# Re-cutting the eight PSUM banks of an encoder layer: three large and two small tiles in place of two and four

## The chip, the cores and the metric

One core of one Trainium2 chip runs the whole program in one launch. Five engines work side by side, each through its own instruction stream in order: PE multiplies matrices and writes only to PSUM, ScalarE (ACT) and VectorE (DVE) read PSUM and do the elementwise work, GpSimd (POOL) works on SBUF alone, and SyncE (SP) issues the DMAs. PSUM here is eight banks of 128 partitions x 512 float32 values, and a program divides them into tiles that are taken and given back. The metric is the device time of one execution in microseconds (us), as a median of several runs.

## What is computed

One layer of an encoder with three gated branches, applied to two requests with the same weights: the "prompt" of 1024 tokens and the "sample" of 512, at width 1024. All of it is float32.

```python
def encoder_layer(x, mem, ...):
    h = rms_norm(x, ln_pre)
    z = h @ w_in                                   # 1024 -> 6400 columns
    (pool_in, pool_gate, q, k, v, attn_gate, xq, x_gate, merge_logits) = split(z)
    pool_out  = multiscale_pool(pool_in, w_pool, pool_scale)
    attn_out  = self_attention(rope(rms(q)), rope(rms(k)), v)      # 8 heads of 64, 2 kv heads
    cross_out = cross_attention(xq, rms_norm(mem, ln_mem), w_mem_kv)   # 4 heads of 128, 256 memories
    branches = (pool_out * silu(pool_gate), attn_out * silu(attn_gate), cross_out * silu(x_gate))
    gates = sigmoid(merge_logits + b_merge)
    merged = sum(gates[n] * (branches[n] @ w_branch[n]) for n in range(3))
    return x + rms_norm(merged @ w_out, ln_post)
```

## The kernel before

**Products in three parts.** Every float32 operand is kept as a high part in a rounded float32 form that PE takes at its fast rate, and a low part that is the rest. `mm3` (L132) makes one product of three matmuls: high by high, high by low, low by high. ACT writes the high part, DVE subtracts for the low one (`split`, L164). A matmul is 128x128 by 128x512 where nothing else is said, and its result fills one bank.

**PSUM tiles.** Two tags share the eight banks. `A` (L91) gives tiles of 1024 values, two banks each, and there are two of them. `B` (L94) gives tiles of 512, one bank each, and there are four. A planner runs over the traced program before it is compiled: it puts each engine's instructions into an order by priority (mostly the order of the source, moved ahead where the code says `tc.high_priority`), hands out tiles of a tag as they come free, and inserts the waits. On the chip the order of each engine is then fixed.

**The stages, in order of time.**

- *Start* (to about 97 us). `mem_phase` (L660) makes keys and values of the memories into A tiles. Between its steps it advances `long_h` (L232), which normalises the prompt's 1024 tokens in two halves: `mean_squares` and `spread` (L209) put each token's factor along a row of 512 in a B tile, and `scaled` (L254) multiplies it in, straight from that B tile (L257). It then builds seven combinations of blocks, `h[0]` to `h[6]`, with DVE subtractions.
- *Block products* (about 68 to 584 us). `products` (L318) takes weight tiles two by two for the prompt and makes their 2x2 blocks with seven block products in place of eight. Each is 12 matmuls. They add into three sums named in the string `"XYXZXZX"` (L363): X takes the products 0, 2, 4 and 6, Y takes 1, Z takes 3 and 5. All three are B tiles (L367). A pair takes about 20 us, X is open all that while, and ACT or DVE reads X in between (`keep`, `both`). After each product one step of a background task runs: tails that transpose k, q and v (A for the first transposes, B named `tp` for the second) and the pooling tail (B named `o`).
- *Bare products of the sample* (about 582 to 690 us). `plain` (L393) makes one product of 24 matmuls at a time into a B tile, for the first pairs of the sample; its tails run as background.
- *Attention* (about 690 to 1148 us). `stream` (L888) steps through units: 64 of the prompt's self-attention, 8 of its cross-attention, 16 pairs of units of the sample, 4 of its cross-attention. For each unit `scores` (L771) takes an A tile, fills it with 4 matmuls, DVE takes the row maximum (L782) and ACT the exponential (L784), which is the last reader. Two units later `turn` (L789) takes an A tile for 8 transposes, and ACT and DVE split it (L800). Two units later again `values` (L802) adds 8 matmuls of 256 columns into a B tile `o` that is held over two units; ACT and DVE read it out (L882, L883). `weave` (L108) puts halves of the sample's remaining `plain` products between the units, as a filling.
- *Merge and output* (about 1156 us to the end), three blocks of 512 tokens. `merge` (L981) makes 24 products of 12 matmuls into B tiles `pj` (L989), which DVE reads at L996. `out_phase` (L1003) takes A tiles for the first half of the columns and B, B and A for the second; `ending` (L1063) finishes the last quarter with a B tile for each of four token tiles (L1073).

Small SBUF tiles of 128x512 come from the tag `hu` (L85, eight buffers), large ones from `med` (fourteen).

Of the kernel before, what the change touches and what calls it, by code (L numbers as in the profile page):

```python
# [61 lines left out]
def encoder_kernel(ctx: ExitStack, tc, wt, xs, xts, mt, cols, rows, rope, edge, ys):  # L62
# [12 lines left out]
    def nm(s):  # L75
        count[0] += 1
        return f"{s}_{count[0]}"
# [11 lines left out]
        return sb.tile([P, D], F32, tag="raw", bufs=NRAW, name=nm("raw"))  # L89

    def A(dt=F32):  # L91
        return ps.tile([P, 1024], dt, tag="A", bufs=2, name=nm("A"))

    def B(dt=F32):  # L94
        return ps.tile([P, 512], dt, tag="B", bufs=4, name=nm("B"))

    def S(n):
        return st.tile([P, n], F32, tag=f"s{n}", bufs=3 if n == 16 else 8, name=nm("s"))
# [110 lines left out]
    def spread(r, out=None):  # L209

        dg = U()[:, :BLK]
        shape = [P, TT, P]
        v.tensor_tensor(dg.rearrange("p (t m) -> p t m", t=TT), ident[:].unsqueeze(1).broadcast_to(shape),
                        r.unsqueeze(2).broadcast_to(shape), op=ALU.mult)
        b = B()
        cost[0] += 3 * BLK / 2.4
        mm(b[:], ones[:], dg, start=True, stop=True)
        if out is None:
            return b[:]
        with tc.high_priority(EVAC):  # L220
            act.activation(out, b[:], AF.Copy)
# [10 lines left out]
    def long_h(xt, h):  # L232

        h += [[None] * 4 for _ in range(7)]
        xv = xt.rearrange("p (k t) -> p k t", k=KC)
        q = [[M(F32) for _ in range(2)] for _ in range(2)]
        for j in range(2):
            for i in range(2):
                load(q[i][j][:].rearrange("p (c n) -> p c n", c=4), xv[:, i * 4:i * 4 + 4, j * BLK:(j + 1) * BLK])
        yield  # L240
        r, sp, sq = S(16), [], []
        for j in range(2):
            sq.append([squares(q[i][j][:]) for i in range(2)])
            yield
        for j in range(2):
            rj = r[:, j * TT:(j + 1) * TT]
            mean_squares(sq[j], rj)
            rstd_of(rj)
            yield
            sp.append(spread(rj))  # L250
            yield
        b11, b12, b21, b22 = [[q[i][j][:, :D], q[i][j][:, D:]] for i in range(2) for j in range(2)]

        def scaled(i, j):  # L254
            for c in range(4):
                x = q[i][j][:, c * BLK:(c + 1) * BLK]
                v.scalar_tensor_tensor(x, x, colt[:, i * 4 + c:i * 4 + c + 1], sp[j], op0=ALU.mult, op1=ALU.mult)  # L257

        def put(k, x):
            for c in range(2):  # L260
                parts_of(h[k], 2 * c, x[c])

        def difference(out, a, b):
            for c in range(2):
                v.tensor_tensor(out[c], a[c], b[c], op=ALU.subtract)

        scaled(0, 0)
        put(0, b11)
        yield
        scaled(1, 0)  # L270
        put(1, b21)
        yield
        scaled(0, 1)
        scaled(1, 1)
        yield
        t3, t4 = (U(), U()), (U(), U())
        difference(t3, b22, b12)
        difference(b12, b12, b11)
        difference(b11, b22, b12)
        put(2, b11)  # L280
        put(3, b12)
        put(4, t3)
        put(5, b22)
        difference(t4, b21, b11)
        put(6, t4)
# [32 lines left out]
    def products(pairs, h, n, background):  # L318

        ops = {}  # L320

        def prepare():
            for p, (k0, k1, _) in enumerate(pairs):
                r0, r1 = RAW(), RAW()
                load(r0[:], wt[TILES[k0]])
                load(r1[:], wt[TILES[k1]])
                a11, a12, a21, a22 = r0[:, :BLK], r0[:, BLK:], r1[:, :BLK], r1[:, BLK:]
                ta, tb = SUM(), SUM()
                s2, s1, s3, s4 = ta[:, :BLK], ta[:, BLK:], tb[:, :BLK], tb[:, BLK:]
                with tc.high_priority(AHEAD):  # L330
                    v.tensor_tensor(s1, a21, a22, op=ALU.add)
                    v.tensor_tensor(s2, s1, a11, op=ALU.subtract)
                    v.tensor_tensor(s3, a11, a21, op=ALU.subtract)
                    v.tensor_tensor(s4, a12, s2, op=ALU.subtract)
                for i, x in enumerate((r0[:], ta[:], tb[:], a22)):
                    hi, lo = [w[:, :x.free_size()] for w in WT()]
                    with tc.high_priority(AHEAD):
                        split(hi, lo, x)
                    for k in range(2 if i < 3 else 1):
                        ops[p, 2 * i + k] = [w[:, k * BLK:(k + 1) * BLK] for w in (hi, lo)]  # L340
                    yield

        prep = prepare()
        done = 0

        def ready(i):
            nonlocal done
            while done < i and next(prep, prep) is not prep:
                done += 1

        for p, (_, _, take) in enumerate(pairs):
            banks = {}
            kept = {}

            def keep(k, b):
                kept[k] = HU()
                with tc.high_priority(EVAC):
                    act.activation(kept[k][:, :n], b, AF.Copy)

            def both(i, j, b, k):  # L360
                take(i, j, b, kept.pop(k)[:, :n])

            for i, bank in enumerate("XYXZXZX"):  # L363
                ready(p * 4 + i // 2 + LOOK)
                start = bank not in banks
                if start:
                    banks[bank] = B()  # L367
                b = banks[bank][:, :n]
                w = ops.pop((p, i))
                for c in range(4):  # L370
                    s = slice(c * P, (c + 1) * P)
                    mm3(b, (w[0][:, s], w[1][:, s]), h[i][c], start and c == 0, c == 3,
                        skip_group_check=True)
                    if c == 1:
                        yield
                if i == 0:
                    keep("p1", b)
                elif i == 1:
                    both(0, 0, b, "p1")
                elif i == 2:  # L380
                    keep("p16", b)
                elif i == 3:
                    keep("p5", b)
                elif i == 4:
                    both(1, 1, b, "p5")
                elif i == 5:
                    both(0, 1, b, "p16")
                else:
                    take(1, 0, b, None)
                next(background, None)  # L390
                yield

    def plain(pairs, h, background):  # L393

        for k0, k1, take in pairs:
            for i, key in enumerate((k0, k1)):
                w, b = weights(*key), B()
                for k in range(KC):
                    mm3(b[:], w(slice(k * P, (k + 1) * P)), h[k], k == 0, k == KC - 1)
                    if k == 3:  # L400
                        next(background, None)
                        yield
                take(i, 0, b[:], None)
                next(background, None)
                yield

    def summed(b, s, out=None):

# [572 lines left out]
    def merge(n, gd, bs, br, acc, merged):  # L981

        if not acc:
            acc += [M(F32), M(F32)]
        for d in range(KC):
            w = weights("branch", n, d // 2) if d % 2 == 0 else w
            sg = HU()
            load(sg[:], gd[n][d][:, bs])
            pj = B()  # L989
            for k in range(4):  # L990
                mm3(pj[:], w(slice((d % 2) * 512 + k * P, (d % 2) * 512 + (k + 1) * P)), br[k], k == 0, k == 3)
            yield
            at = acc[d // 4][:, (d % 4) * BLK:(d % 4 + 1) * BLK]
            with tc.high_priority(EVAC):
                o = at if n == 0 else sg[:]
                v.scalar_tensor_tensor(o, sg[:], 1.0, pj[:], op0=ALU.add, op1=ALU.mult)  # L996
            if n > 0:
                pool.tensor_tensor(at, at, sg[:], op=ALU.add)  # L998
            if merged is not None and d % 2:
                merged.extend(split_pair(acc[d // 4][:, (d % 4 - 1) * BLK:(d % 4 + 1) * BLK]))  # L1000
            yield
# [61 lines left out]
    def ending(merged, src, dst, yv, ssq, lnpost):  # L1063
# [6 lines left out]
        for t in range(TT):  # L1070
            x = U()
            load(x, src[t * P:(t + 1) * P, :])
            o = B()[:, :256]  # L1073
            for k in range(KC):
                ts = slice(t * P, (t + 1) * P)
                s = slice(k % 4 * 256, k % 4 * 256 + 256)
# [24 lines left out]
    run(drained(products(pairs[-4:], h, BLK, bg)))  # L1101
    run(pre)
    scs, kts, vts, pairs, bg, _, drained = group(0)
    run(plain(pairs[0], hs, bg))
    merged = []
    fill = drained(plain(pairs[1], hs, bg))
    units = [u for b in range(2) for u in attention(b, sc, kt, vt)]
    units += [u for b in range(2) for u in cross(b, sc, mkd[1], mvd[1])]
    units += pairs_of(scs, kts, vts) + cross(0, scs, mkd[0], mvd[0])
# [103 lines left out]
```

## Time and profile before

| | |
|---|---|
| median of three runs | 1495.29 us (1495.1 to 1495.49) |
| profiled execution, device time | 1496.65 us |
| its span, first to last instruction | 1494.8 us |
| work outside that span | 1.85 us |
| mean granted TensorE clock | 0.989 |
| PE busy / weight loads (PEld) | 1456.0 us / 1210.1 us |
| DVE / ACT / POOL busy | 976.5 / 709.6 / 273.3 us |

A row of a group or of the timeline gives engine, line, operation, tile written <- tiles read, shape and count. Matmuls overlap: one of 512 columns is shown with some 390 ns, while the next starts about 0.23 us after it, so starts tell more than lengths. PEld is the load of a matmul's stationary operand, which runs ahead of the matmul. Brackets at the end of a timeline row, and the last column of the waits, tell how long an engine was idle and what ended it.

### The profile page before, as it was taken

To read this page: it belongs to the slowest core of one execution; us is meant where nothing else is said; L and a number is where in the kernel's file an instruction comes from. 1 tells how busy PE (TensorE), PEld (TensorE's weight loads), DVE (VectorE), ACT (ScalarE), POOL (GpSimd) and SP (SyncE) were. 2 spreads that over 40 slices of the span, in tenths; PEclk is the share of its full clock that TensorE was granted. 3 is DMA by queue.
4 is the path that set the end of the run, shared out by engine and by line. 5 is a ranking of instruction groups with operands and counts; after the bars stand their busy time and mean duration, and the time that the engine had idled before them with its cause. 6 is when DMAs were issued, how large, how long until landed. Compare 5 with 4: busy or idle time off the path is not lost.

```text
span 1494.8 us, 19564 instructions
## 1 busy us (share of the span) xinstructions
PE 1456.0 (97%) x7264; PEld 1210.1 (81%) x7264; DVE 976.5 (65%) x1215; ACT 709.6 (47%) x1083; POOL 273.3 (18%) x286
## 2 busy tenths in 40 slices
PE   7979999999999999999999999999998999999998
PEld 5768888888888888887888888888886888888887
DVE  6996586666648564747767666676775664764764
ACT  6444444544434545434656556566675233323332
POOL 1000020110000000301222222234232150250241
PEclk9989999999999999999999999999999999999999
DMA  7513233332422434344222223165446844954952
GB/s 277 172 47 106 85 114 125 108 132 66 129 92 78 158 133 128 102 150 148 64 96 80 91 68 106 58 219 173 155 155 214 286 148 132 347 193 140 336 163 84
DMA packets 88174, 211.37 MB, mean 141 GB/s; under 512 B 9872, under 2 KB 19216, under 8 KB 87312
## 3 DMA queue, kind: packets, MB, share of 16 engines
q1 hardware_dynamic: 88080, 210.14, 42.7%
q8 instruction: 57, 0.93, 0.3%
q14 instruction: 37, 0.30, 0.1%
HBM read 155.57 MB, written 54.53 MB: 141 GB/s over the span
## 4 chain that ended last, share of the span: by engine, by line
PE 85%; DMA 4%; DVE 4%; ACT 4%; issue 2%; SPq 1%; POOL 0%; DVEq 0%; POOLq 0%; ACTq 0%
PE B L126 66%; PE A L126 14%; PE A L130 5%; ACT u L784 1%; DVE s L782 1%; ACT whi L165 1%; DMA raw<-wt 1%; DVE wlo L162 1%; PE B L130 1%; DMA hu<-xq 1%; ACT med L165 1%; SPq L139 1%; DMA u<-x_prompt 0%; DMA hu<-merge 0%; DMA hu<-x_gate 0%
## 5 line engine op out<-in xcount | busy, mean ns | idle before, releaser
L126 PE MATMUL B<-med,whi 128*128 128x512 f32 x2776 | 871.2, 394 | 15.8 <-ACT med L165 15.8
L126 PEld LDWEIGHTS B<-med,whi 128*128 128x128 f32 x2776 | 515.8, 189 | 122.2 <-ACT med L165 17.5
L126 PE MATMUL B<-med,wlo 128*128 128x512 f32 x1388 | 544.1, 392 | 0.6 <-DVE wlo L162 0.6
L126 PEld LDWEIGHTS B<-med,wlo 128*128 128x128 f32 x1388 | 261.9, 189 | 56.6 <-DVE wlo L162 1.7
L162 DVE TENSOR_TENSOR wlo<-raw,whi 128x1024 fp32r<-128x1024 f32 (+1 forms) x169 | 213.3, 1263 | 141.6 <-ACT whi L165 140.7
L165 ACT ACTIVATE whi<-raw 128x1024 fp32r<-128x1024 f32 (+1 forms) x169 | 167.5, 991 | 288.5 <-PE B L126 198.3
L165 ACT ACTIVATE med<-A 128x1024 fp32r<-128x1024 f32 x92 | 94.3, 1025 | 108.4 <-PE A L130 108.2
L162 DVE TENSOR_TENSOR med<-A,med 128x1024 fp32r<-128x1024 f32 (+1 forms) x93 | 113.0, 1215 | 42.0 <-ACT med L165 40.8
L187 POOL TENSOR_SCALAR s<-s 128x16 f32<-128x16 f32 (+3 forms) x17 | 6.9, 404 | 669.0 <-DVE s L556 333.2
L786 POOL TENSOR_SCALAR u<-u,s 128x1024 f32<-128x1024 f32 x64 | 72.1, 1127 | 251.3 <-DVE s L785 219.1
L130 PE MATMUL A<-ident,u 128*128 128x128 f32 x784 | 102.8, 273 | 0.9 <-DVE med L162 0.2
L130 PEld LDWEIGHTS A<-ident,u 128*128 128x128 f32 x784 | 90.1, 140 | 16.3 <-issue 5.2
L998 POOL TENSOR_TENSOR med<-med,hu 128x512 f32<-128x512 f32 x48 | 77.0, 1617 | 142.3 <-DVE hu L996 142.2
L782 DVE TENSOR_REDUCE s<-A 128x1 f32<-128x1024 f32 x64 | 78.1, 1220 | 32.9 <-PE A L126 11.3
L126 PE MATMUL A<-kt,med 128*128 128x512 f32 x320 | 91.9, 409 | 2.7 <-ACT u L784 1.2
L126 PE MATMUL A<-whi,med 128*128 128x512 f32 (+1 forms) x320 | 92.4, 368 | 0.2 <-ACT hu L1027 0.2
L784 ACT ACTIVATE u<-A,s 128x1024 f32<-128x1024 f32 x64 | 71.3, 1114 | 38.4 <-DVE s L782 38.0
L165 ACT ACTIVATE whi<-sum 128x1024 fp32r<-128x1024 f32 x50 | 53.1, 1062 | 65.6 <-PE B L126 63.7
L162 DVE TENSOR_TENSOR med<-med,med 128x1024 fp32r<-128x1024 f32 (+1 forms) x50 | 55.8, 1127 | 38.1 <-ACT med L165 34.2
L165 ACT ACTIVATE med<-med 128x1024 fp32r<-128x1024 f32 (+1 forms) x44 | 44.2, 1017 | 74.8 <-POOL med L998 36.2
L162 DVE TENSOR_TENSOR wlo<-sum,whi 128x1024 fp32r<-128x1024 f32 x50 | 61.1, 1221 | 23.3 <-ACT whi L165 22.4
L126 PE MATMUL B<-med,vt 128*128 128x256 f32 x512 | 75.9, 287 | 0.4 <-ACT med L165 0.4
(179 smaller groups left out, 1610.4 us busy)
## 6 DMA issues: line engine op xcount, KB each, us to landing
raw<-wt SPq DMA_DIRECT2D x168, 512.0 KB, 3.7
merge<-hu SPq DMA_DIRECT2D x72, 256.0 KB, 2.0
hu<-merge SPq DMA_DIRECT2D x72, 256.0 KB, 5.2
med<-br SPq DMA_DIRECT2D x36, 256.0 KB, 5.6
q<-hu SPq DMA_DIRECT2D x24, 256.0 KB, 2.6
br<-hu SPq DMA_DIRECT2D x24, 256.0 KB, 2.3
med<-q SPq DMA_DIRECT2D x12, 512.0 KB, 5.0
med<-xt_prompt SPq DMA_DIRECT2D x4, 1024.0 KB, 13.2
```

Source lines behind the costliest of these rows:

```text
L126: pe.matmul(out, l, r, **k)
L130: pe.transpose(out, x, i[:])
L139: return nc.sync.dma_start(out, src)
L162: v.tensor_tensor(out, x, hi.bitcast(F32), op=ALU.subtract)
L165: act.activation(hi, x, AF.Copy)
L187: pool.tensor_scalar(ss, ss, EPS, 1.0, op0=ALU.add, op1=ALU.mult)
L782: v.reduce_max(mx[:], a[:], axis=AX.X, negate=True)
L784: act.activation(p, a[:], AF.Exp, bias=mx[:], accum_out=sm[:])
L786: pool.tensor_scalar(p, p, rc[:], 1.0, op0=ALU.mult, op1=ALU.mult)
L998: pool.tensor_tensor(at, at, sg[:], op=ALU.add)
```

## The change

Five edits, all on who takes which PSUM tile. The tag A gets three tiles and B two: again eight banks. In `long_h` the spread factors are copied by ACT into an `hu` tile each and `scaled` reads them there. In `products` X takes the first half of an A tile, Y and Z stay with B. `plain` gets its tile from a function that the caller passes: before the attention B and A in turn, within it always B. `merge` and `ending` take B and A in turn.

```diff
     def A(dt=F32):
-        return ps.tile([P, 1024], dt, tag="A", bufs=2, name=nm("A"))
+        return ps.tile([P, 1024], dt, tag="A", bufs=3, name=nm("A"))
 
     def B(dt=F32):
-        return ps.tile([P, 512], dt, tag="B", bufs=4, name=nm("B"))
+        return ps.tile([P, 512], dt, tag="B", bufs=2, name=nm("B"))
...
             yield
-            sp.append(spread(rj))
+            sp.append(HU())
+            spread(rj, sp[j][:])
             yield
...
-                v.scalar_tensor_tensor(x, x, colt[:, i * 4 + c:i * 4 + c + 1], sp[j], op0=ALU.mult, op1=ALU.mult)
+                v.scalar_tensor_tensor(x, x, colt[:, i * 4 + c:i * 4 + c + 1], sp[j][:], op0=ALU.mult, op1=ALU.mult)
...
                 if start:
-                    banks[bank] = B()
-                b = banks[bank][:, :n]
+                    banks[bank] = (A() if bank == "X" else B())[:, :n]
+                b = banks[bank]
...
-    def plain(pairs, h, background):
+    def plain(pairs, h, background, bank):
...
-                w, b = weights(*key), B()
+                w, b = weights(*key), bank(i)
...
+    def single(i):
+        return B()
+
+    def either(i):
+        return (A() if i % 2 else B())[:, :BLK]
...
-            pj = B()
+            pj = either(d)
...
-            o = B()[:, :256]
+            o = either(t)[:, :256]
...
-    run(plain(pairs[0], hs, bg))
+    run(plain(pairs[0], hs, bg, either))
     merged = []
-    fill = drained(plain(pairs[1], hs, bg))
+    fill = drained(plain(pairs[1], hs, bg, single))
```

## The prediction

> **What bounds the kernel now.** I read the page first, then the busy time by stage.
>
> ```profile
> span 1494.8 us, 19564 instructions
> PE 1456.0 (97%) x7264; PEld 1210.1 (81%) x7264; DVE 976.5 (65%) x1215; ACT 709.6 (47%) x1083; POOL 273.3 (18%) x286
> core 0: us, PE busy (x) PEld busy (x) DVE busy (x) ACT busy (x) POOL busy (x), PEclk, DMA share, GB/s
> 97.00:690.00 593.00, 592.83 (x2730) 488.50 (x2730) 379.72 (x518) 263.46 (x377) 43.45 (x41) 1.00 0.35 113
> 690.00:990.00 300.00, 296.21 (x1741) 248.97 (x1740) 202.72 (x250) 179.51 (x262) 81.14 (x77) 1.00 0.29 94
> 990.00:1148.00 158.00, 156.74 (x945) 135.31 (x944) 112.22 (x141) 108.22 (x245) 58.63 (x91) 1.00 0.53 170
> ```
>
> PE is the bound in these stages, at full clock. In the products, block and bare, it is idle for 0.2 of 593 us; more tiles can win nothing there. But a busy PE hides short waits, because a matmul is drawn long after the next could have begun. So I looked at what the weight loads waited for in the attention, 690 to 1148 us, where both tags are in heavy use. The first four rows are the loads' waits, the last two the matmuls' own (total us, times, longest):
>
> ```profile
> PEld A L126 <- ACT u L784: 11.5, 29, 0.8
> PEld A L130 <- issue: 5.2, 14, 0.5
> PEld A L126 <- DVE med L162: 3.6, 11, 1.0
> PEld A L126 <- ACT u L931: 0.5, 1, 0.5
> PE A L126 <- ACT u L784: 1.4, 7, 0.4
> PE A L126 <- DVE med L162: 0.6, 1, 0.6
> ```
>
> Nearly all are for A. Scores wait until an exponential (L784) or the split of a turned tile (L162) has read an A tile out. One such wait in the timeline, loads, matmuls, and ACT:
>
> ```profile
> 904.02 0.19 PEld L126 LDWEIGHTS B<-med,wlo 128*128 128x128 f32 x1
> 904.25 0.42 PEld L126 LDWEIGHTS B<-med,whi 128*128 128x128 f32 x2
> 905.28 0.76 PEld L126 LDWEIGHTS A<-kt,med 128*128 128x128 f32 x4 [0.61 <-ACT u L784]
> 904.25 0.40 PE L126 MATMUL B<-med,wlo 128*128 128x512 f32 x1
> 905.28 1.19 PE L126 MATMUL A<-kt,med 128*128 128x512 f32 x4 [0.18 <-ACT u L784]
> 904.03 1.12 ACT L784 ACTIVATE u<-A,s 128x1024 f32<-128x1024 f32 x1 [0.25 <-DVE s L782]
> ```
>
> A load normally starts 0.23 us before its matmul (904.02, 904.25), while the matmul before it runs. Here load and matmul both start at 905.28, once the exponential has ended at 905.15. So 0.61 us of idle loads cost about 0.61 - 0.23 = 0.38 us of matmul time, of which the matmul's own row shows 0.18.
>
> **The change part by part.**
>
> *The third A tile in the attention.* It removes the waits above. Worked like the example: 11.5 + 3.6 + 0.5 = 15.6 us in 41 waits, less 41 x 0.23 = 9.4, gives **-6.2 us**. From below the matmuls' own idle is 1.4 + 0.6 = 2.0 us; from above, all idle of the loads is 15.6. I take 6.2, which is nearest to what the example shows. The 14 waits "issue" are before turns (L130) and show no releaser, so I leave them: A tiles may be in them, up to 5.2 - 14 x 0.23 = 2.0 us more. What is late next? For a unit DVE needs a maximum and a subtraction, ACT an exponential and a rounding:
>
> ```profile
> L782 DVE TENSOR_REDUCE s<-A 128x1 f32<-128x1024 f32 x64 | 78.1, 1220 | 32.9 <-PE A L126 11.3 <-issue 10.5 <-POOL u L786 7.5
> L784 ACT ACTIVATE u<-A,s 128x1024 f32<-128x1024 f32 x64 | 71.3, 1114 | 38.4 <-DVE s L782 38.0
> L165 ACT ACTIVATE med<-A 128x1024 fp32r<-128x1024 f32 x92 | 94.3, 1025 | 108.4 <-PE A L130 108.2
> L162 DVE TENSOR_TENSOR med<-A,med 128x1024 fp32r<-128x1024 f32 x92 | 112.3, 1220 | 41.0 <-ACT med L165 40.8
> ```
>
> 64 units fill about 300 us, 4.7 each. With one tile for scores (matmuls 1.19, then 1.22 and 1.11) and one for the turn (transposes 1.0, then 1.02 and 1.22) a unit keeps A tiles for 3.5 + 3.2 = 6.7 us: 71% of two tiles, 48% of three. DVE is busy for 202.72 of 300 us and ACT for 179.51, so PE stays the bound.
>
> *Two B tiles in the attention.* Here the change can add waits. `o` holds a B tile over two units and a filling product another. I followed every B tile from its first matmul to its last reader: in 690 to 1148 us never more than three are held, and 13 times a third begins before one of two is read out, 9.9 us early in total. The first, one from the middle, and the last:
>
> ```profile
> 705.72 0.75 DVE L655 SCALAR_TENSOR_TENSOR hu<-B,colt,med 128x512 f32<-128x512 f32 x1 [0.36 <-PE B L126]
> 706.08 0.39 PE L126 MATMUL B<-med,vt 128*128 128x256 f32 x1
> ...
> 895.73 0.28 PE L126 MATMUL B<-med,vt 128*128 128x256 f32 x1
> 896.85 0.42 DVE L883 TENSOR_TENSOR hu<-B,hu 64x256 f32<-64x256 f32 x1
> 897.79 1.07 PE L126 MATMUL B<-med,vt 128*128 128x256 f32 x7
> ...
> 1144.21 4.37 PE L126 MATMUL B<-med,med 128*128 128x512 f32 x18
> 1147.87 0.69 DVE L957 TENSOR_TENSOR hu<-B,hu 128x512 f32<-128x512 f32 x1 [0.90 <-DMA hu<-x_gate]
> ```
>
> At 895.73 a new `o` gets one early matmul while the last is read until 897.27 and a product is open; with two tiles that matmul has to come 1.5 us later. But the other seven come at 897.79 anyway, and PE has the product's matmuls to put there. So most of the 9.9 us is covered by other matmuls already in the stream; uncovered it costs all of it. I price each place like an average A wait, 6.2 / 41 = 0.15 us: 13 x 0.15 = 2.0. As four of them (of 1.3 to 1.5 us each) look like 895.73, where one matmul moves, I take **+1.5 us**, ends 0 and 9.9. Behind a waiting `o` on PE stand the next scores and the filling, and behind these ACT and DVE.
>
> *Block products.* X holds an A tile for 20 us and the next X overlaps it by some 3 us; a tail takes one A for 5 us. At most three are wanted at once. Y, Z and the tails' tiles never want a third B. Here a large tile is half used. [...] **0**, ends 0 and +2.
>
> *Bare products before the attention* take B and A in turn; the tails' transposes use B.
>
> ```profile
> 617.62 0.47 PE L130 MATMUL B<-identr,med 128*128 128x128 f32 x4
> 618.80 1.07 ACT L414 ACTIVATE med<-B 128x512 f32<-128x512 f32 x2
> ```
>
> A product that would be in B begins 0.3 us after these transposes, while the last but one, also in B, is read by the first L414 until about 619.3. Three such places, to 625 us, want a third B, by 1 to 1.5 us each. The product in A can go first: 3 x 0.15, **+0.5**, ends 0 and 4.
>
> *Start.* Added are two ACT copies like L221; L257 then reads SBUF as L311 does:
>
> ```profile
> L221 ACT ACTIVATE hu<-B x2: 597/598/598, 32.8 to 525.0; 128x512 f32<-128x512 f32 x2
> L257 DVE SCALAR_TENSOR_TENSOR med<-med,colt,B x16: 739/742/744, 42.9 to 69.2; 128x512 f32<-128x512 f32 x16
> L311 DVE SCALAR_TENSOR_TENSOR u<-u,colt,hu x8: 743/748/749, 526.7 to 538.0; 128x512 f32<-128x512 f32 x8
> 44.96 1.06 ACT L165 ACTIVATE med<-med 128x1024 fp32r<-128x1024 f32 x1 [3.53 <-DVE med L257]
> ```
>
> 16 x 6 ns = **+0.1**. The copies, 1.2 us, lie where ACT waits anyway (3.5 us before 44.96). Uncovered they delay the DVE chain that PE waits for before 83 us; the two `hu` tiles could also hold back the memories' evacuations. Ends -0.5 and +1.5.
>
> *Merge and output.* Five tiles taken in turn in place of four. The third A matters once: the last quarter's A tile need not wait for the evacuation.
>
> ```profile
> PE A L126 <- ACT hu L1027: 0.2, 1, 0.2
> ```
>
> **-0.2**, ends -0.4 and +1.
>
> *End of the attention.* The 18 matmuls at 1144.21 are three cross units, one B tile each. The third would wait for L957 to end at 1148.56, 1.5 us. It delays that unit's store, and with it the second half of the loads that `merge` begins with; the first half is queued on SP before it. **+0.3**, ends 0 and 1.5.
>
> Sum: -6.2 + 1.5 + 0 + 0.5 + 0.1 - 0.2 + 0.3 = **-4.0 us**, so the profiled span would be 1490.8 us. The profiled execution took 1496.65 us, 1.4 above the median of 1495.29; the same difference gives a median of **1491.3 us**, 0.27% less.
>
> **The rivals.**
>
> *The wait only changes its tag* (B waits as A did). For it: in a span of six units `o` is open for most of the time, and so is a product, so two B tiles are about as full as two A tiles were. Against it: B is taken about 0.8 times a unit (half an `o` and a third of a product), A twice. If B gives back 4 to 8 us, the time is 1493 to 1497; middle 1495.
>
> *Slower: two B tiles close the filling.* A product can't begin until the last one is read out unless `o` is free, and PE, in order, stands. Place: each handover of `o` or a product while both are open. Price: the 9.9 us in full, 4 before the attention, 1.5 at its end: -6.4 + 9.9 + 4 + 1.5 + 0.1 = +9, or 1504. It turns the sign once more than about half of these early starts reach PE. A longer stop costs more, as after the start's wait:
>
> ```profile
> 25.76 0.79 PE L126 MATMUL A<-mh,whi 128*128 128x512 f32 x1 [2.81 <-ACT whi L165]
> 28.46 0.63 PE L126 MATMUL A<-mh,wlo 128*128 128x512 f32 x1
> 28.89 0.63 PE L126 MATMUL A<-mh,whi 128*128 128x512 f32 x1
> ```
>
> After 2.81 us of idle, matmuls start 0.43 us apart in place of 0.23. [...] As PE finds cover for some of it, I put this case at 1499 to 1503, middle 1501.
>
> *More than the waits.* With A free the planner can run attention further ahead of the filling, and filling left over would cover the 7.05 us in which PE waits for the first merge:
>
> ```profile
> 1155.62 2.06 PE L126 MATMUL B<-med,whi 128*128 128x512 f32 x3 [7.05 <-ACT med L165]
> ```
>
> That gives up to -7 more, 1484. Against it: the filling is woven in by the source's cost account, which does not change.
>
> *It does not do what it says*: scores wait for ACT itself and not for a tile. Then the time is 1495. Against it, scores read only q and keys, both long there, so L784 can hold them back by the tile alone.
>
> **How the numbers follow.** Forecast 0.47, the wait changes its tag or nothing comes 0.27, slower 0.17, more 0.09. The forecast's own range is 1488 to 1493.5. The range to hold 8 in 10 leaves out the upper half of the slow rival and the far end of the good one: **1485 to 1500**. A measurement of this kernel can tell about 0.2% (3 us) from no change, so faster means below 1492.3: most of the forecast (0.40) and the good rival (0.09), in sum 0.49. Slower means above 1498.3: 0.17. Same: 0.34.
>
> **What would show it.** Right: the loads' waits for A on L784 and L162 in the attention fall from 15.1 us to under 4; the stage from 690 to 1148 shortens by 4 to 6 us; products keep their length within 1 us. Wrong: new waits of PE or PEld for B on L883, L479, L464 or L957 (second and third rival), gaps within 97 to 690 us, a later first product than 68 us or a longer stop before 83 us. The forecast fails most easily by the B handovers, whose cover I judged from one order of instructions that the planner will lay out anew.

## The result, and the profile after

The changed kernel takes **1485.55 us** in the median of four runs (1484.2 to 1487.24), against 1495.39 of the kernel before. The ratio is 0.9932, with a 95% interval of 0.9915 to 0.995. Run again later it gave 1484.8 us and 0.9936 (0.9923 to 0.9948). The forecast was 1491.3: the way was right, the gain is 9.8 us in place of 4. The time lies below the forecast's own range of 1488 to 1493.5, and only 0.55 us inside the range of 1485 to 1500.

The page of the changed kernel, its span and the engines' busy time, and then the busy time by stage, the attention being 10 us shorter:

```profile
span 1484.1 us, 19530 instructions
PE 1447.6 (98%) x7264; PEld 1212.4 (82%) x7264; DVE 972.4 (66%) x1215; ACT 713.1 (48%) x1085; POOL 275.8 (19%) x286
...
97.00:690.00 593.00, 590.92 (x2718) 486.18 (x2717) 377.63 (x515) 261.66 (x375) 42.07 (x41) 1.00 0.35 112
690.00:990.00 300.00, 298.20 (x1797) 257.96 (x1795) 206.18 (x256) 186.42 (x271) 82.98 (x79) 1.00 0.32 102
```

PE did 1797 matmuls from 690 to 990 us where it had done 1741. Below are all waits of the weight loads from 690 to 1160 us in the changed kernel. A wait counts there when it is over 0.15 us. The changed kernel's code lines behind `plain` stand seven further down: L464 is now L471, L784 L791, L883 L890, L957 L964, L996 L1003.

```profile
PEld A L130 <- issue: 6.6, 14, 2.2
PEld B L126 <- ACT med L165: 3.6, 1, 3.6
PEld B L126 <- issue: 2.4, 1, 2.4
PEld B L126 <- DVE hu L471: 1.4, 3, 0.5
PEld A L126 <- DMA med<-q: 1.3, 2, 0.8
PEld B L126 <- DVE hu L890: 1.3, 4, 0.4
PEld B L126 <- DVE med L162: 0.8, 1, 0.8
PEld B L126 <- DVE hu L964: 0.4, 2, 0.2
```

The 29 waits for an A tile on the exponential are gone, and so are the 11 on the split. The 14 waits "issue" ahead of turns are still 14, one of them now 2.2 us long. In place of the others stand a few for B (read out at L471 by a gate, at L890 for `o`), and one before the first merge. The matmuls' own waits add two stops of 2 us (before 1140 us) that were not there:

```profile
PE B L126 <- DVE hu L964: 2.0, 1, 2.0
PE A L130 <- issue: 2.0, 1, 2.0
```

The stages, by the start of their first matmuls in the traces of all runs (us; one profiled execution each). Rows are named by the experiments below.

| kernel | first block product | block products | bare products | first scores to first merge | first merge to end |
|---|---|---|---|---|---|
| before | 68.23 | 513.75 | 110.37 | 463.27 | 339.22 |
| changed | 68.35 | 513.07 | 111.66 | **452.88** | 338.19 |
| changed, again | 66.63 | 512.73 | 111.80 | 453.17 | 338.19 |
| 2 A, 2 B | 68.36 | 512.39 | 111.57 | **463.98** | 340.86 |
| 2 A, 4 B | 68.20 | 513.07 | 110.07 | **462.46** | 338.37 |
| sums swapped | 68.64 | 513.53 | 111.42 | 453.66 | 337.33 |
| merge in B alone | 68.23 | 513.23 | 111.61 | 453.33 | **357.19** |
| spread in PSUM | 67.55 | 514.45 | 111.51 | 454.60 | 336.99 |
| cross values in turn | 67.58 | 512.61 | 111.53 | 455.54 | 339.96 |
| filling in turn | 66.62 | 513.55 | 111.92 | **458.78** | 337.48 |
| bare products in B | 67.91 | 513.54 | **119.10** | 452.94 | 337.14 |
| changed, share 0.64 | 68.89 | 512.90 | 111.70 | **444.07** | 337.62 |
| changed, share 0.61 | 67.90 | 512.90 | 111.55 | **449.17** | 335.25 |
| before, share 0.64 | 68.24 | 513.47 | 109.90 | **458.97** | 338.88 |

### The profile page after: what moved, and what is told of

It is laid out like the page before. It is cut to its first block, busy times and chain, and to the rows that moved or that the text cites. A ratio compares the mean times of both kernels' runs of the same rounds, so it can differ in the third digit from the quotient of the medians.

```text
span 1484.1 us, 19530 instructions
## 1 busy us (share of the span) xinstructions
PE 1447.6 (98%) x7264; PEld 1212.4 (82%) x7264; DVE 972.4 (66%) x1215; ACT 713.1 (48%) x1085; POOL 275.8 (19%) x286
## 4 chain that ended last, share of the span: by engine, by line
PE 89%; DVE 3%; DMA 3%; issue 1%; ACT 1%; SPq 1%; POOL 1%; DVEq 0%; POOLq 0%; ACTq 0%
PE B L126 42%; PE A L126 41%; PE A L130 5%; DVE wlo L162 1%; DMA raw<-wt 1%; SPq L139 1%; PE B L130 1%; DMA hu<-wt 1%; DMA hu<-merge 1%; DVE med L162 1%; POOL s L191 0%; ACT whi L165 0%; ACT med L165 0%; DVE med L266 0%; DMA med<-q 0%
## 5 line engine op out<-in xcount | busy, mean ns | idle before, releaser
L126 PE MATMUL B<-med,whi 128*128 128x512 f32 x1544 | 483.6, 393 | 5.7 <-ACT med L165 4.4
L126 PE MATMUL A<-med,whi 128*128 128x512 f32 x1232 | 386.9, 394 | 6.9 <-ACT med L165 6.7
L126 PEld LDWEIGHTS B<-med,whi 128*128 128x128 f32 x1544 | 286.6, 188 | 64.9 <-ACT med L165 5.4
L162 DVE TENSOR_TENSOR wlo<-raw,whi 128x1024 fp32r<-128x1024 f32 (+1 forms) x169 | 213.5, 1264 | 162.8 <-ACT whi L165 149.5
L126 PE MATMUL B<-med,wlo 128*128 128x512 f32 x772 | 302.4, 392 | 0.5 <-DVE wlo L162 0.5
L126 PEld LDWEIGHTS A<-med,whi 128*128 128x128 f32 x1232 | 230.7, 189 | 55.6 <-ACT med L165 7.4
L126 PE MATMUL A<-med,wlo 128*128 128x512 f32 x616 | 241.2, 392 | 0.3 <-DVE wlo L162 0.3
L126 PEld LDWEIGHTS B<-med,wlo 128*128 128x128 f32 x772 | 145.2, 188 | 32.0 <-DVE wlo L162 1.3
L162 DVE TENSOR_TENSOR med<-A,med 128x1024 fp32r<-128x1024 f32 (+1 forms) x93 | 113.1, 1216 | 39.5 <-ACT med L165 37.8
L126 PEld LDWEIGHTS A<-med,wlo 128*128 128x128 f32 x616 | 116.3, 189 | 25.6 <-DVE wlo L162 0.9
L126 PE MATMUL A<-whi,med 128*128 128x512 f32 (+1 forms) x352 | 98.3, 360 | 0.0
L126 PE MATMUL A<-kt,med 128*128 128x512 f32 x320 | 88.6, 396 | 0.5 <-DMA med<-q 0.4
L791 ACT ACTIVATE u<-A,s 128x1024 f32<-128x1024 f32 x64 | 71.3, 1114 | 29.7 <-DVE s L789 27.3
```

The costliest lines, as they stand in the source:

```text
L126: pe.matmul(out, l, r, **k)
L162: v.tensor_tensor(out, x, hi.bitcast(F32), op=ALU.subtract)
L791: act.activation(p, a[:], AF.Exp, bias=mx[:], accum_out=sm[:])
```

## The experiments

Medians and ratios are against runs of the kernel before on the same chip (1494.3 to 1494.7 us).

**Is it the third A tile, or the new routing?** Both kernels keep the routing of the change. The first takes the third large tile away and leaves two banks unused; the second also gives the two small tiles back. In the two expectations the stretches are written 200 us too short: 252.9 stands for 452.9, 263.3 for 463.3, and so with the others.

```diff
-        return ps.tile([P, 1024], dt, tag="A", bufs=3, name=nm("A"))
+        return ps.tile([P, 1024], dt, tag="A", bufs=2, name=nm("A"))
```

> The changed kernel with two large tiles in place of three, two small ones, two banks unused: the third large tile alone is taken away. Theory (scores wait for a large tile, and each such wait costs the first scores matmul some 0.27 us and the second another 0.10): the weight loads' waits on the exponential and on the split of turned tiles come back to 12 to 18 us, about half or more of the 64 first units start their second scores matmul over 60 ns late, the stretch from the first scores to the first merge goes from 252.9 back to 262 to 267 us (263.3 before), and the kernel takes 1494 to 1500 us. Rival (the gain came from the new routing of tiles and the order that the planner made of it, not from the tile itself): the stretch stays at 252 to 256 us and the kernel at 1485 to 1489.

```diff
-        return ps.tile([P, 1024], dt, tag="A", bufs=3, name=nm("A"))
+        return ps.tile([P, 1024], dt, tag="A", bufs=2, name=nm("A"))
...
-        return ps.tile([P, 512], dt, tag="B", bufs=2, name=nm("B"))
+        return ps.tile([P, 512], dt, tag="B", bufs=4, name=nm("B"))
```

> The changed kernel with two large and four small tiles as before: only the routing of the tiles is left of the change. Theory: the large tiles' waits stay, stretch 261 to 265 us, kernel 1493 to 1499 (block products may lose up to 3 us, since two first sums and a tail want three large tiles at once some six times). Against e1 it shows what two small tiles cost in the attention: I expect 2 to 5 us, the rival of the prediction (small tiles as full as large ones) 6 to 10. Rival of e1: 1485 to 1489.

With 2 A and 2 B: 1498.98 us, ratio 1.0034 (1.0022 to 1.0046). With 2 A and 4 B: 1496.34, 1.001 (1.0001 to 1.002). The waits of the loads for A in the attention, first with two B, then with four:

```profile
PEld A L126 <- ACT u L791: 11.1, 26, 0.8
PEld A L126 <- DVE med L162: 2.6, 9, 0.5
```

```profile
PEld A L126 <- ACT u L791: 11.4, 29, 0.8
PEld A L126 <- DVE med L162: 3.0, 11, 0.4
```

All is back, and the routing alone wins nothing. By the stage table the third A, at two B each, is worth 463.98 - 452.88 = **11.1 us**, and going from four B to two, at two A each, costs 463.98 - 462.46 = **1.5 us**, less than the 2 to 5 expected. The rival of these runs has fallen. Two banks left empty cost no more than these 1.5 us and 2.5 us behind the first merge.

**Filling in both tags.** If B were now the narrow place, moving filling products to A should help.

```diff
-    fill = drained(plain(pairs[1], hs, bg, single))
+    fill = drained(plain(pairs[1], hs, bg, either))
```

> The changed kernel with the attention's filling products in small and large tiles in turn. It takes load from the two small tiles and puts it on the three large ones: a filling product keeps its tile about 12 us. Theory (large tiles are what the attention lacks): waits on small tiles go (some 3 to 5 us of PE time), waits on large ones come back while a filling product is in one, half of the time, and the kernel takes 1486 to 1492 us. Rival (small tiles are now the narrow place): 1481 to 1484.

1490.58 us, ratio 0.9974 (0.9964 to 0.9983), within what the theory gave. The stage grows to 458.78 us, and waits on L791 come back:

```profile
PEld A L126 <- ACT u L791: 6.9, 11, 1.2
```

Five of these 11 are ahead of scores, four of them while a filling product is in an A tile. The other six are ahead of a filling product itself, which now has to wait until the scores give an A tile back. So the third A is worth its price only while the filling keeps out of it.

**The stop of 2.05 us for a small tile at the end of the attention.**

```diff
-            o = B()
+            o = either(c)
             for m in range(2):
```

> The changed kernel in which the cross-attention's values take small and large tiles in turn. In the changed kernel the last but one unit's values stand 2.05 us for a small tile that is read out late (a gate's load). If that stop is on the path that ends in the first merge, the first merge begins 1.5 to 2 us earlier after the last filling product and the kernel takes 1483 to 1484.5 us; if the merge waits for its loads anyway, 1485 to 1486.

1489.11 us, ratio 0.9969 (0.9956 to 0.9982): slower than the changed kernel, which neither side expected. The stop is gone, but the next one is longer. The waits of PE around the end, changed kernel (from 1140 us) and then this one:

```profile
PE B L126 <- ACT med L165: 3.1, 1, 3.1
PE B L126 <- DVE hu L964: 2.0, 1, 2.0
```

```profile
PE B L126 <- ACT med L165: 7.0, 1, 7.0
PE B L126 <- DVE hu L890: 0.2, 1, 0.2
```

The first merge waits for a chain: gate loads, the evacuation at L964, its store, then the merge's loads, which stand behind that store on SP. The stop for B lay inside that wait. One piece of the chain of waits (start, us) in the changed kernel, then in this one:

```profile
1136.03 2.96 DMA hu<-x_gate
```

```profile
1136.80 0.43 SPq L139
1137.27 4.18 DMA hu<-x_gate
```

Here the gate load that counts is issued later and takes longer, so the chain ends later still. The order on SP explains which load counts. Around the stores of L965, changed kernel and then this one:

```profile
1139.73 1.01 SPq L965 DMA_DIRECT2D br<-hu  x2
1140.80 0.46 SPq L139 DMA_DIRECT2D med<-br  x1
```

```profile
1139.37 3.25 SPq L965 DMA_DIRECT2D br<-hu  x4
1142.67 1.42 SPq L139 DMA_DIRECT2D med<-br  x3
```

In the changed kernel the load that the merge needs stands behind two of the four stores; here it stands behind all four and is issued 1.9 us later. Why the planner chose this order was not tried.

**Which sum of a block product sits in the large tile.**

```diff
-                    banks[bank] = (A() if bank == "X" else B())[:, :n]
+                    banks[bank] = (B() if bank == "X" else A())[:, :n]
```

> The changed kernel with the block product's first sum X in a small tile and the other two in large ones, counts as changed. X is open for a whole pair of 20 us and overlaps the next X, so both small tiles are taken for some 3 us a pair and one for the rest. Theory (the block products have no wait because X has three large tiles): tails' second transposes, which need a small tile, wait or push the products, and the stage from first to last block product (513.1 us in the changed kernel) grows by 1 to 6 us; kernel 1486 to 1492. Rival (any split will do, since PE has always other matmuls): stage within 0.5 us, kernel 1484.5 to 1487.

1487.39 us, ratio 0.9953 (0.9938 to 0.9968), block products 513.53 us. The rival holds for the stage, which does not care; the kernel is 0.4 us above the rival's range, but its interval overlaps that of the changed kernel. PE is idle for only 0.3 of the 485 us from 97 to 582 us, so it has other matmuls there nearly always.

**Merge in small tiles alone.**

```diff
-            pj = either(d)
+            pj = B()
...
-            o = either(t)[:, :256]
+            o = B()[:, :256]
```

> The changed kernel with merge and the last quarter in small tiles only, two of them. A merge product is 12 matmuls, 2.7 us, and is read out by one DVE instruction of 0.7 us, so two tiles should do: kernel 1485 to 1487, first merge to end within 1 us of 338.2. Rival (the turn between the two tags is needed): a stop of 0.3 us or more for many of the 72 products, 20 us or more, kernel over 1500.

1506.5 us, ratio 1.009 (1.0071 to 1.0109): 19 us more from the first merge to the end. My theory fell; the turn between the tags is needed, though not for the reason that the rival gave. Stops of PE over 2 us, in this kernel:

```profile
PE B L126 <- DVE med L1003: 7.8, 2, 3.9
PE B L126 <- DVE hu L1003: 2.4, 2, 2.1
```

The two of 3.9 us lie where one block's output meets the next block's merge. The one of 2.09 us lies in the second block's merge, where the read-out stands behind a split (L162) on DVE. DVE, in order, around the first of them:

```profile
1267.09 2.48 DVE L1027 SCALAR_TENSOR_TENSOR u<-med,s,u 128x1024 f32<-128x1024 f32 x2 [1.10 <-POOL s L191]
1269.48 0.68 DVE L1003 SCALAR_TENSOR_TENSOR med<-hu,B 128x512 f32<-128x512 f32 x1
```

The read-out of a merge product (L1003) stands behind the output's last step (L1027), which waits for POOL. With two tiles PE has no third to go on into. With five, taken in turn, it runs on: behind the first merge the changed kernel's PE waits 0.5 us in all. After two of the three stops the granted clock was 0.50 for the 3.3 us of the rows below, here under an undisturbed stretch at 1.00 (the clock is the number before the DMA share):

```profile
1262.00:1266.00 4.00, 4.00 (x19) 3.32 (x18) 3.98 (x6) 1.50 (x5) 0.00 (x0) 1.00 0.53 165
1271.20:1274.50 3.30, 3.30 (x10) 2.52 (x9) 0.95 (x1) 0.00 (x0) 0.00 (x0) 0.50 1.05 400
1329.20:1332.50 3.30, 3.30 (x8) 2.56 (x9) 2.23 (x2) 0.00 (x0) 3.30 (x2) 0.50 0.16 10
```

The three stops make matmuls 10.4 us late. Half the clock for 3.3 us after each would cost about 5 us more (3 x 3.3 / 2), an estimate that takes the third stop to be like the two shown. Most of the rest of the 19 us is in stops of up to 1 us.

**The spread factors back in PSUM.**

```diff
-            sp.append(HU())
-            spread(rj, sp[j][:])
+            sp.append(spread(rj))
```

(`scaled` then reads `sp[j]` itself, as before.)

> The changed kernel with the prompt's spread factors read from the small tile again, without the two ACT copies. Prediction's step: the copies cost nothing, so the first block product begins at 68.3 +- 0.5 us as now and the kernel takes 1485 to 1487. Rival: both small tiles are taken until about 70 us, the second one of a block product then waits, first stop before 83 us longer, kernel 1487 to 1490.

1486.97 us, ratio 0.9949 (0.9935 to 0.9964). The first block product starts at 67.55 us, a little ahead of the 67.8 to 68.8 expected but within the spread of this start over all runs (66.6 to 68.9), and the block products take 514.45 us, 1.4 more. The copies cost nothing, as said; whether they win that 1.4 us is not settled, since the two intervals overlap.

**Bare products in small tiles alone.**

```diff
-    run(plain(pairs[0], hs, bg, either))
+    run(plain(pairs[0], hs, bg, single))
```

> The changed kernel with the bare products before the attention in small tiles only. Two small tiles then carry products (6 us each, read out some 1.4 us later, up to 8 us where a large buffer is waited for) and the tails' transposes. Theory: the stage from the first bare product to the first scores, 111.7 us as changed and 110.4 before, grows by 3 to 10 us, kernel 1488 to 1495. Rival (PE finds other work): 1485 to 1487.

1492.69 us, ratio 0.9992 (0.9982 to 1.0002): the stage grows by 7.4 us to 119.10 and eats nearly the whole gain. So here, too, two small tiles are short as soon as products and tails share them.

**The filling's share.** The last filling matmul starts 13.5 us before the first merge (14.7 before the change). Two runs move the filling later with one constant, beside the changed kernel again.

> The changed kernel itself, once more, as the measure for the two beside it: 1484 to 1487 us, ratio to before 0.993 to 0.995.

```diff
-LAG, VLAG, SHARE, LOOK, WAIT = 2, 2, 0.66, 1, 6
+LAG, VLAG, SHARE, LOOK, WAIT = 2, 2, 0.64, 1, 6
```

> The changed kernel with the filling woven in at a share of 0.64 in place of 0.66. In the changed kernel the last filling matmul starts 13.5 us before the first merge, and PE then stands 2.0 and 3.1 us in two places. Theory (the end of the attention is a chain of loads and read-outs that only leftover filling can cover): the filling ends 3 to 8 us later, the stretch from the first scores to the first merge is 1 to 3 us shorter than 452.9, kernel 1482 to 1485. Rival (the planner pulls filling forward wherever PE has room, so the share decides little): within 1 us of the changed kernel beside it.

> The same with a share of 0.61. Theory: the filling lasts to the end of the attention and beyond, and what is left runs while the merge waits for its loads: stretch 449 to 452 us, kernel 1481 to 1484. Against it: if more filling is left than the gap holds, the scores of the last units come closer together than ACT and DVE can follow, PE waits there, and the kernel is at 1485 or above.

At 0.64: **1475.85 us**, ratio 0.9875 (0.986 to 0.989), 9 us less than the changed kernel beside it. At 0.61: 1479.9, 0.9902 (0.9889 to 0.9916). The theory holds for the way and was too small by far (at 0.61 the stretch of 449.17 us is within what it gave, the kernel 1.1 us below): the rest of the filling now stands between the last cross units, and the first merge follows them with no stop. Of the 8.8 us by which the stretch is shorter at 0.64, the two stops at the end are 5.4. Another 1.8 us come from turns, where the stop near 990 us is gone, and 0.9 from `o`: these have to do with the order of the instructions and not with the end. The filling ends only 1.3 us later, counted from the first scores, where 3 to 8 were expected. The timeline of PE at 0.64:

```profile
1134.13 0.39 PE L126 MATMUL B<-med,wlo 128*128 128x512 f32 x1
1134.36 1.52 PE L126 MATMUL B<-med,med 128*128 128x512 f32 x6
1136.07 1.66 PE L126 MATMUL B<-med,med 128*128 128x512 f32 x6 [0.19 <-ACT hu L486]
1137.56 1.21 PE L126 MATMUL A<-med,whi 128*128 128x512 f32 x3
```

At 0.61 filling is left over when the last unit ends, and is run 0.23 us before the first merge begins; the stage is 5 us longer again. The last run asks whether this gain belongs to the share alone: the kernel before, with 0.64.

> The kernel before, with the filling's share at 0.64 and nothing else changed. If the 9 us of the share (changed kernel 1484.8, with 0.64 1475.9) have nothing to do with the tiles, the stop of 7.05 us ahead of the first merge goes here too: fill end to first merge 14.7 to about 3.5 us, kernel 1485 to 1489. If they come from the third large tile, which lets attention's end run closer together, the stretch from first scores to first merge stays at 459 to 464 us and the kernel at 1491 to 1495.

1491.29 us, ratio 0.9977 (0.9967 to 0.9986). The end closes here too (last filling to first merge 4.2 us), but the stage only falls by 4.3 us to 458.97, where the changed kernel's fell by 8.8. The loads wait for A as before:

```profile
PEld A L126 <- ACT u L784: 11.6, 33, 1.0
PEld A L126 <- DVE med L162: 4.4, 12, 0.7
```

So the result lies between the two answers that I had written down: part of the share's gain needs no new tiles, part does. At a share of 0.64 the tiles are worth 458.97 - 444.07 = 14.9 us in the stage, at 0.66 10.4.

## Why the prediction was right, and its sums were not

**How far it was luck.** The mechanism and the place are right, the size is not. By the balance below, A gave 12.7 us where 6.2 were counted, and B took back 5.3 where 1.8 were counted (1.5, and 0.3 at the end); the two errors partly cancel, and the time stayed inside the range of 1485 to 1500 by 0.55 us. Of the signs written down, the waits for A fell to none, the stage shortened by 10.4 us in place of 4 to 6, and some signs of "wrong" appeared as well: waits for B on L890, L964 and L471 (L883, L957 and L464 before the change).

**The bound and the place: right.** PE bounds the kernel, its products could win nothing (513.75 to 513.07 us), and the gain came in the attention, where scores had waited for A tiles. The 2 A kernels show that nothing else in the change brings it.

**The price of a wait: the step that was mis-sized.** The prediction took 15.6 us of idle loads, subtracted 0.23 us of ordinary lead for each of 41 waits, and called the rest, 6.2, the cost. It priced the late start of the first matmul after a wait and stopped there. The second starts late too: here the load that has waited starts together with its matmul (905.28), and this matmul is shown with 0.50 us in place of 0.40. The first scores matmul after a wait and then the first two (kernel before), and two without a wait (changed kernel):

```profile
905.28 0.50 PE L126 MATMUL A<-kt,med 128*128 128x512 f32 x1 [0.18 <-ACT u L784]
905.28 0.73 PE L126 MATMUL A<-kt,med 128*128 128x512 f32 x2 [0.18 <-ACT u L784]
```

```profile
912.67 0.63 PE L126 MATMUL A<-kt,med 128*128 128x512 f32 x2
```

That is 0.10 us, and it is lost once: the second load starts at 905.39, again 0.23 us ahead of its matmul. From the starts of all 80 scores in self-attention of both requests, against the 0.227 us that normally lie between starts (waits over 0.15 us; in each row but the last one wait is for the load of q, in the last both are):

| kernel | scores whose load waited | first matmul late, sum | second late, sum | second late by over 0.06 |
|---|---|---|---|---|
| before | 36 of 80 | 6.0 us | 3.67 us | 33 of 36 |
| 2 A, 4 B | 36 | 5.5 | 3.61 | 33 of 36 |
| 2 A, 2 B | 31 | 5.0 | 3.19 | 30 of 31 |
| filling in turn | 9 | 1.9 | 0.94 | 9 of 9 |
| changed | 2 | 0.8 | 0.23 | 2 of 2 |

The group of scores matmuls shows the same on both pages, and before also 1.2 us of idle on the exponential:

```profile
L126 PE MATMUL A<-kt,med 128*128 128x512 f32 x320 | 91.9, 409 | 2.7 <-ACT u L784 1.2 <-DMA med<-q 0.9
```

```profile
L126 PE MATMUL A<-kt,med 128*128 128x512 f32 x320 | 88.6, 396 | 0.5 <-DMA med<-q 0.4
```

Shorter waits cost this too: before the change 13 more scores, whose loads had waited 0.09 to 0.14 us, have a second matmul that is over 0.06 us late.

**The balance of the stage.** From the same starts, first scores to first merge, changed less before: the first of a unit's scores -6.1 us, as priced (though the 6.2 had six waits ahead of the cross units' scores in it); the following ones -4.3, not priced; scores of the cross units -2.3; `o` in B +2.6; cross values in B +2.7; turns +1.0, with one new stop of 2.0 us near 990 us; filling and first merge -4.0, nearly all from the shorter stop before the first merge, 7.05 to 3.14 us. Sum -10.4 us.

The trace names no releaser for the new stop, but its timeline points at A again, now with three tiles. ACT, and then the transposes that had waited:

```profile
991.74 0.23 ACT L938 ACTIVATION_READ_ACCUMULATOR u<-A,s 128x1 f32 x1
992.06 1.06 PE L130 MATMUL A<-ident,u 128*128 128x128 f32 x8 [2.00 <-issue]
```

One A tile was being split until 992.31, one held the scores of the next cross unit, and the third was the one that ACT had finished reading at 991.97. That this set the transposes free was not tried.

**Two B tiles: right when alone, too small beside three A.** The forecast +1.5 us is what the pair of 2 A kernels measured, but the agreement is partly luck. The forecast saw the loss mainly at the handovers of `o` and of products. In the pair, by the same starts, `o` and the filling products lose 2.5 us, cross values 1.1 and turns 0.6; 2.1 come back as a shorter stop ahead of the first merge, and 0.5 at the scores. With A free `o` and the cross values lost 5.3 us by the balance, presumably because the small tiles are asked for more closely. Part of the rival "the wait changes its tag" came true; it took less than half of what A gave. A stop of the cross units for B I had foreseen (1.5 us, for the last of them; it came with 2.05 us at the last but one), and had put on the chain only in part; the run with cross values in turn shows that taking it away wins nothing.

**The end of the attention: wrong sign.** I expected +0.3 us and got 1.2 us less from the last filling to the first merge (14.70 to 13.49). The rival that leftover filling would cover the stop did not come about by itself: the filling ended even earlier relative to the last unit. The share runs show that the mechanism is real, and worth 5.4 of the 9 us that moving the constant wins.

**The small terms.** Block products 0, measured -0.7. Bare products +0.5, measured +1.3. PE has one wait between 580 and 690 us, on the read-out of a product, at the place that the prediction named:

```profile
PE B L126 <- ACT med L421: 1.3, 1, 1.3
```

Start +0.1, measured +0.1, though the same program's start differs by over 1 us between two runs. Merge and output -0.2, measured -1.0, below the lower end of -0.4; I had not asked what the turn itself is worth, 19 us.

**The slower rival** did not come. It needed more than half of the B handovers to reach PE. But the runs with merge and bare products in B alone show its price where two small tiles are all there is: 19 and 7 us.

## What to carry to other kernels

Price a wait of a pipelined engine by the starts of the next few instructions, up to the point where they are in step again, and not by the idle time of the first. When a buffer goes from one tag to another, look at every stage that lived on the old count, and give those stages both tags in turn: here the tile that the attention needed would have cost more in the merge than it won. After such a change set the constants of the order anew; the same share moved the old kernel by 3.4 us and the new one by 9.

## What the runs showed of the hardware

Where the load of a scores matmul had waited, the next matmul was late by about 0.10 us more: 3.67 us over 36 scores before, 3.61 over 36 with 2 A and 4 B, 3.19 over 31 with 2 A and 2 B, and 0.94 over 9 with the filling in turn.

A stop of PE in the run with merge in B alone:

```profile
1329.07 1.09 PE L126 MATMUL B<-med,whi 128*128 128x512 f32 x2 [2.09 <-DVE hu L1003]
```

These 2.09 us were followed by a clock of 0.50 from 1329.2 to 1332.5 us, and a stop of 3.9 us ahead of 1270.3 us by one of 0.50 from 1271.2 to 1274.5. In the changed kernel the clock was 1.00 from 988 to 999 us, around the stop of 2.0 us near 990 us. Why two stops of nearly the same length differ is not shown: no run was made to test it.
